# Moving the summing of adaLN modulation rows to VectorE, and into later stages, in a two-layer diffusion trunk

## The chip, the cores and the metric

The kernel runs on 1 core of one Trainium2 chip. The metric is the device time of one execution, in microseconds (us). Engines are called TensorE (PE, its weight loads PEld), VectorE (DVE), ScalarE (ACT), GpSimd (POOL) and SyncE (SP, which issues most transfers).

## What is computed

A trunk of two layers over 1024 latent tokens and 256 context tokens with 1024 features. Layer 0 mixes with a gated short convolution and latent attention, layer 1 with banded windowed attention; each layer ends in a mixture of 16 experts. Every sub-layer is shifted, scaled and gated by modulation rows: six rows of 1024 values per layer, for latent tokens (from `c`) and, where they are needed, for context tokens (from `c_ctx`). Cut to this:

```python
mod = jax.nn.silu(c) @ mod_w[layer] + mod_b[layer]            # 1024 -> 6 x 1024
sh1, sc1, g1, sh2, sc2, g2 = jnp.split(mod[:, None, :], N_MOD, axis=-1)
modc = jax.nn.silu(c_ctx) @ mod_w[layer] + mod_b[layer]       # the same for the context
h = modulate(rms_norm(xs, norm1_g[layer]), sh1, sc1)          # rows 0, 1
...                                                           # y: the mixer of h and hc
xs = xs + g1 * y                                              # row 2
h2 = modulate(rms_norm(xs, norm2_g[layer]), sh2, sc2)         # rows 3, 4
xs = xs + g2 * ec_moe(h2, ...)                                # row 5
```

`mod_w` is 2 x 1024 x 6144 in float32, 50 MB: each row of a layer is a product of one vector with a 4 MB matrix.

## The kernel before

The program runs in stages, one after the other: layer 0's input projection with the convolution (`layer0_conv`), latents, latent attention, output projection with router (`mixer_out`), experts of layer 0 (`moe`), then the same for layer 1.

**Modulation rows.** A row is the sum over 1024 inputs of weight times `silu(c)`. There are two ways to make one. `Part` takes two rows at a time for both kinds of tokens on TensorE: eight pieces of 128 inputs x 2048 features (1 MB each), each used by four products of 32 x 512 (`Part.use`, L299). `Row` takes one row on VectorE: a piece holds 2 x 128 inputs x 1024 features (1 MB); for each 128 inputs and kind of tokens one operation multiplies 128 x 1024 weights by a value per partition and adds them to an accumulator `modacc` (L348; L350 for the first). At its end a few products with ones add over the partitions (`Row.sum`, L356), the bias `modb` is added and GpSimd's queue stores the row in `modr`. The first two rows of layer 0 are a `Part` before everything else. The rest, rows 2 to 5 of layer 0 and 0 and 1 of layer 1 as three `Part`s, and rows 2 to 5 of layer 1 as four `Row`s for latent tokens alone, is a generator (`modulations`), advanced by one piece after nearly every projection of the convolution (`next(rest, None)` in `proj`), with its weights loaded two pieces ahead into the common ring of 1 MB buffers (`raw`).

**Convolution.** Four chunks of 384 columns; per chunk and group of 256 tokens three projections of 24 products each (`pc`), read by ScalarE or VectorE from four PSUM banks. Written order on every queue (`manual_schedule`).

**Output projection.** Tiles of 128 tokens, written order on every queue. In `steps(j)` a tile's 48 products `pw` come in two halves. Beside them run: for the tile before, `xn` of its second half (L1202, L1203), its store to `acc_x`, nine products later its transposes (L1237), then the norm (`nss` to `rr`, eleven short operations), `mul` (L1218), `add` (L1222), store of `h2x`; for the tile itself `xn` of the first half, once the first 24 products are done, and nine products later the first transposes of that. `yl` is the split of the next tile's input. Tile 1 has one more operation, `o.scale(0)`.

**Experts of layer 0.** Per expert twelve weight chunks of 1 MB. Each is loaded into the ring (seven buffers in this stage), cast by ScalarE (`wh`, L1080) and its rest made by VectorE (`wl`, L1081), four buffers deep, and used by three products per block (`pg`, `pu`, `pd`). Context tokens use the raw chunk itself (`pcg`, `pcd`), which frees it. `sil`, `hl`, `xl`, `yo` are VectorE's other operations. In this loop the order on each queue is set by the scheduler, which places instructions by priority in the order of the program and by a model of when their operands are ready. `early()` reads layer 1's rows 0, 1, 3, 4 back at expert 1.

Of the kernel before, what the change touches and what calls it, by code (L numbers as in the profile page):

```python
# [21 lines left out]
D = 1024  # L22
# [17 lines left out]
# one step of the software pipeline of an attention: (operation, how many steps late)  # L40
# [55 lines left out]
def hybrid_block_kernel(ctx, tc, A, out, dbg=None, upto=99):  # L96
# [13 lines left out]
    def psum(name, **tags):  # L110
        """PSUM of a phase: tag -> (buffers, banks each)"""
# [21 lines left out]

    warm = const.tile([128, 1], F32, name="warm")
# [32 lines left out]
    def rstd_steps(pool_, ss, n, dim, tag, out=None):  # L167
        """1/sqrt(ss/dim + eps) for ss [128, n]: the root of dim times 1/sqrt(ss + dim*eps). A generator"""
# [42 lines left out]
    def scale_rows(pool_, l, s, i, g):  # L211
        """norm_g * (1 + sc) on all partitions"""
# [8 lines left out]
    def columns(c, n, scratch, tag):  # L221
        """n rows of D features with the features on partitions: c [128, row, 8]"""
# [4 lines left out]
    class Ring:  # L227
        """buffers for what is read from DRAM, in turn"""
# [4 lines left out]
        def more(self, raws):  # L233
            """further buffers, next in turn"""
# [11 lines left out]
    class Ahead:  # L246
        """the output projection of the first layer in four parts, the first of them split ahead"""
# [29 lines left out]
    class Part:  # L277
        """two of the rows, for latent and context tokens, 512 features at a time, summed by TensorE"""
# [31 lines left out]
        def units(self):  # L310
            def load(k):
                if k == 5:
                    self.load_b()
                self.load(k)

            def use(k):
                self.use(k)
                if k == 7:
                    self.sum()
                    self.store()  # L320

            return [(partial(load, k), partial(use, k)) for k in range(8)]

    class Row:
        """one of the rows, for the kinds of tokens ss, summed by VectorE but over the partitions"""

        def __init__(self, c, l, r, ss, pool_):
            self.c, self.l, self.r, self.ss, self.pool = c, l, r, ss, pool_
            self.w = {}

        def load(self, k):
# [5 lines left out]
            w = self.w[k] = ring.tile([128, 2, D])  # L337
            sp.dma_start(w, A["mod_w"][self.l, k * 128:(k + 2) * 128, self.r * D:(self.r + 1) * D].rearrange("(k p) n -> p k n", p=128))

        def use(self, k):  # L340
# [3 lines left out]
            for i in range(2):  # L344
                for s, a in zip(self.ss, self.acc):
                    cv = self.c[:, 2 * (k + i) + s:2 * (k + i) + s + 1]
# [5 lines left out]
        def sum(self):  # L352
            n = 64 * len(self.ss)
            pm, mb = bank("C", "pm"), self.mb
# [8 lines left out]
        def units(self):  # L363
            return [(partial(self.load, k), partial(self.use, k)) for k in range(0, 8, 2)] + [(None, self.sum)]

    def modulations(parts, rows, ahead):
        """a generator that stops after every piece of the weights, loaded some pieces ahead"""
        a, b = [[u for x in xs for u in x.units()] for xs in (parts, rows)]
        todo = sorted([((i + 0.5) / len(x), i, u) for x in (a, b) for i, u in enumerate(x)], key=lambda t: t[0])
        todo = [u for _, _, u in todo]  # L370
# [15 lines left out]

    def transposes8(src, n=8):
        """eight [128,128] blocks of src (free) into two banks"""
# [8 lines left out]
    # ================= layer 0: projections =================  # L397
    def layer0_conv(hp, wp, cp):
        """first norm, input projection and short convolution"""
        hT = [[hp.tile([128, 8, 256], F32R, name=f"hT{g}_{i}") for i in range(2)] for g in range(5)]  # L400
        csil = hp.tile([128, 16], F32, name="csil")
# [9 lines left out]
        class Group:  # L411
            """256 tokens"""
# [14 lines left out]
            def norm(self):  # L427
                """a generator"""
# [16 lines left out]
            def T(self, b, tag="B"):  # L445
                """two blocks of 128 features of the normalized tokens, features on partitions"""
# [26 lines left out]
        class Chunk:  # L473
            """columns of the input projection, 256 features at a time"""
# [23 lines left out]
        def aside():  # L498
            """the next of the small operations that run between others"""
# [55 lines left out]
        rest = modulations([Part(cs, l, i, cp) for l, i in PARTS], [Row(csil, l, r, ss, cp) for l, r, ss in ROWS], 2)  # L555
# [1874 lines left out]
```

## Time and profile before

| | us |
|---|---|
| median of 3 runs | 2926.6 (2924.9 to 2929.13) |
| span of the profiled execution | 2924.6 |
| TensorE busy | 2732.1 (93%) |
| VectorE busy | 2126.5 (73%) |
| ScalarE busy | 1609.2 (55%) |
| GpSimd busy | 443.8 (15%) |

The profiled execution's own time is its span, 2924.6, and what lies around it, about 2 us by the median. Busy time of TensorE is modelled, so a full TensorE is not TensorE at its peak. The granted clock is a share of 2.4 GHz: 1.00 is that, 0.50 is 1.2 GHz. Start times are from the span's start.

### The profile page before, as it was taken

The page shows a single profiled execution, that of the slowest core. Times are in us where ns is not written, and L with a number is a line of the kernel's source. Part 1 is how long each engine was busy: PE and PEld are TensorE (multiplying, and loading weights), DVE is VectorE, ACT ScalarE, POOL GpSimd, SP SyncE. Part 2 cuts the span into 40 slices and gives each one's busy share as a digit, 9 for nine tenths or more (in the row PEclk, how much of TensorE's full clock was granted, in tenths as well). Part 3 has the DMA queues.
Part 4 walks back from the last instruction along what each step waited for, and adds up shares of the span by engine and source line. Part 5 has one row for each costly group of instructions (what it writes and reads, how often), then busy time and mean ns, then how long its engine had stood idle before and what let it go on. Part 6 is the DMA issues. An engine that isn't in the chain of part 4 may idle for free. (4 is left out here: it accounts for less than half of the span.)

```text
span 2924.6 us, 43411 instructions
## 1 busy us (share of the span) xinstructions
PE 2732.1 (93%) x16999; PEld 2160.2 (74%) x16999; DVE 2126.5 (73%) x3298; ACT 1609.2 (55%) x2390; POOL 443.8 (15%) x293
## 2 busy tenths in 40 slices
PE   6999899999959999999999899899998599999996
PEld 5889899988746666666666678688877488877775
DVE  4653799986666666666666554799976688888887
ACT  4201577773225555555555543588943377776664
POOL 2100100000050111010011210232200622221103
PEclk8999999999979999999999999799999799999998
DMA  7782000016438878788888631310056599999994
GB/s 266 286 317 88 5 8 10 9 60 232 159 111 311 290 275 276 273 290 273 276 270 276 227 126 73 128 37 30 25 192 239 197 377 384 383 382 370 367 354 144
DMA packets 274637, 613.91 MB, mean 210 GB/s; under 512 B 25064, under 2 KB 72928, under 8 KB 270336
## 3 DMA queue, kind: packets, MB, share of 16 engines
q1 hardware_dynamic: 259408, 567.38, 54.2%
q0 software_dynamic: 14880, 43.62, 5.8%
q8 instruction: 134, 2.20, 0.3%
q14 instruction: 71, 0.58, 0.1%
q10 hardware_dynamic: 144, 0.13, 0.0%
HBM read 549.41 MB, written 61.67 MB: 209 GB/s over the span
## 5 line engine op out<-in xcount | busy, mean ns | idle before, releaser
L1081 DVE TENSOR_TENSOR wl<-raw,wh 128x2048 fp32r<-128x2048 f32 (+1 forms) x382 | 861.9, 2283 | 247.7 <-ACT wh L1080 247.6
L1080 ACT CAST wh<-raw 128x2048 fp32r<-128x2048 f32 (+1 forms) x392 | 735.5, 1903 | 260.9 <-PE pg L1723 150.2
L1719 PE MATMUL pg<-wl,xh 128*128 128x512 f32 x512 | 210.0, 410 | 3.6 <-ACT xh L159 2.9
L1721 PE MATMUL pu<-wl,xh 128*128 128x512 f32 x512 | 206.1, 402 | 5.3 <-DVE wl L1081 5.3
L1720 PE MATMUL pg<-wh,xh 128*128 128x512 f32 x512 | 203.2, 397 | 0.0
L1724 PE MATMUL pu<-wh,xl 128*128 128x512 f32 x512 | 202.5, 395 | 0.0
L1723 PE MATMUL pg<-wh,xl 128*128 128x512 f32 x512 | 201.8, 394 | 0.0
L1722 PE MATMUL pu<-wh,xh 128*128 128x512 f32 x512 | 201.6, 394 | 0.0
L1775 PE MATMUL pd<-wl,hh 128*128 128x512 f32 x480 | 197.1, 411 | 1.2
L1776 PE MATMUL pd<-wh,hh 128*128 128x512 f32 x480 | 194.0, 404 | 0.0
L1664 POOL DMA_INDIRECT xg<-h2x,gp x32 | 56.5, 1766 | 721.9 <-PE ptr L393 710.1
L1779 PE MATMUL pd<-wh,hl 128*128 128x512 f32 x480 | 151.2, 395 | 0.0
L1739 ACT ACTIVATE sil<-pg 128x512 f32<-128x512 f32 x64 | 38.3, 598 | 204.3 <-PE pg L1723 204.3
L163 PE MATMUL pc<-hT,wh 128*128 128x256 f32 x480 | 139.8, 291 | 5.5 <-ACT wh L487 3.8
L1789 POOL DMA_INDIRECT acc_x<-yo,gp x30 | 92.9, 3096 | 312.4 <-DVE yo L1788 302.2
L164 PE MATMUL pc<-hT,wh 128*128 128x256 f32 x480 | 135.0, 281 | 0.0
L165 PE MATMUL pc<-hT,wl 128*128 128x256 f32 x480 | 134.9, 281 | 0.0
L1719 PEld LDWEIGHTS pg<-wl,xh 128*128 128x128 f32 x512 | 96.5, 188 | 44.9 <-issue 21.6
L1736 PE MATMUL pcg<-raw,cT 128*32 128x256 f32 x2048 | 125.5, 384 | 0.5 <-DMA raw<-in_exp_w_up_dram 0.5
L1775 PEld LDWEIGHTS pd<-wl,hh 128*128 128x128 f32 x480 | 90.1, 188 | 43.6 <-issue 18.9
L1721 PEld LDWEIGHTS pu<-wl,xh 128*128 128x128 f32 x512 | 96.7, 189 | 32.8 <-DVE wl L1081 10.8
L943 ACT CAST pt<-ppt 128x512 fp32r<-128x512 f32 (+1 forms) x192 | 95.1, 516 | 39.0 <-PE ppt L936 36.8
(437 smaller groups left out, 6638.4 us busy)
## 6 DMA issues: line engine op xcount, KB each, us to landing
raw<-in_exp_w_gate_dram SPq DMA_DIRECT2D x128, 1024.0 KB
raw<-in_exp_w_up_dram SPq DMA_DIRECT2D x128, 1024.0 KB
raw<-in_exp_w_down_dram SPq DMA_DIRECT2D x128, 1024.0 KB
raw<-in_mod_w_dram SPq DMA_DIRECT2D x48, 1024.0 KB
yT<-yTd SPq DMA_DIRECT2D x17, 512.0 KB
acc_x<-xn SPq DMA_DIRECT2D x16, 512.0 KB
h2x<-h SPq DMA_DIRECT2D x16, 512.0 KB
raw<-in_w_in_dram SPq DMA_DIRECT2D x8, 768.0 KB
```

The lines of the kernel that those rows point to most:

```text
L163: pe.matmul(o, ah, bl, start=first, stop=False)
L1080: act.copy(wh[:, cs], raw[:, cs])
L1081: (eng or dve).tensor_sub(wl[:, cs], raw[:, cs], wh[:, cs].bitcast(F32))
L1719: pe.matmul(pg, xh[:, k], gl[:, j], start=k == 0, stop=False)
L1720: pe.matmul(pg, xh[:, k], gh[:, j], start=False, stop=False)
L1721: pe.matmul(pu, xh[:, k], ul[:, j], start=k == 0, stop=False)
L1722: pe.matmul(pu, xh[:, k], uh[:, j], start=False, stop=False)
L1723: pe.matmul(pg, xl[:, k], gh[:, j], start=False, stop=k == 7)
L1724: pe.matmul(pu, xl[:, k], uh[:, j], start=False, stop=k == 7)
L1775: pe.matmul(pd[n], hh[k // 4][:, k % 4], w[2][:, k % 2, ns], start=k == 0, stop=False)
L1776: pe.matmul(pd[n], hh[k // 4][:, k % 4], w[1][:, k % 2, ns], start=False, stop=False)
L1779: pe.matmul(pd[n], hl[k // 4][:, k % 4], w[1][:, k % 2, ns], start=False, stop=k == 7)
```

## The change

`Part` stays for the first two rows alone. All others become `Row`s, spread over three stages:

- convolution: rows 3, 4, 2 of layer 0, for both kinds of tokens, 1 MB pieces, two ahead; the generator is advanced by two of seven projections instead of by each;
- output projection: row 5 of layer 0, for both kinds, in pieces of 128 inputs (512 KB) through one buffer `modw`, one ahead; advanced twice per tile from tile 1 on;
- experts of layer 0: rows 0, 1 (both kinds) and 3, 4, 2, 5 (latent) of layer 1, pieces of 1 MB from the expert ring, one ahead; advanced three times per expert from expert 1 on. Accumulators and bias lie in tiles that the last expert needs later (`lent`). `early()` moves from expert 1 to expert 13.

```diff
-PARTS = [(0, 1), (0, 2), (1, 0)]
-ROWS = [(1, r, (0,)) for r in (2, 3, 4, 5)]
+ROWS = [(3, (0, 1)), (4, (0, 1)), (2, (0, 1))]
+ROWS_OUT = [(5, (0, 1))]
+ROWS_NEXT = [(0, (0, 1)), (1, (0, 1)), (3, (0,)), (4, (0,)), (2, (0,)), (5, (0,))]
...
-            w = self.w[k] = ring.tile([128, 2, D])
+            w = self.w[k] = self.tile([128, self.n, D])
...
-            for i in range(2):
+            for i in range(self.n):
...
-        rest = modulations([Part(cs, l, i, cp) for l, i in PARTS], [Row(csil, l, r, ss, cp) for l, r, ss in ROWS], 2)
+        rest = modulations([Row(0, r, ss, cp, ring.tile, "C") for r, ss in ROWS], 2)
+        calls = [0]
...
                 if j or g > 1:
-                    next(rest, None)
+                    calls[0] += 1
+                    if calls[0] % 7 in (1, 4):
+                        next(rest, None)
...
+            mods = iter(())
+            if l == 0:
+                def mod_tile(shape):
+                    return wp.tile(shape, F32, tag="modw", bufs=1, name="modw")
+
+                mods = modulations([Row(0, r, ss, wp, mod_tile, "B", 1) for r, ss in ROWS_OUT], 1)
...
+                next(mods, None)
                 for _ in range(9):
                     next(m0)
                     yield
+                next(mods, None)
                 y.T(1)
...
+            mods = modulations([Row(1, r, ss, lent, W.tile, "B") for r, ss in ROWS_NEXT], 1) if l == 0 else iter(())
...
+                        if e and c:
+                            steps(mods, 1)
...
-                if e == 1 and early:
+                if e == 13 and early:
...
+                if e:
+                    steps(mods, 1)
                 wd = [W.get(pool if e == E - 1 and c % 2 else None) for c in range(4)]
```

Three places show what moves. First TensorE in the convolution, at the end of a projection and the start of the next; `pm` is a piece of a `Part`, `pc` the projection. Before:

```order
L163 MATMUL pc<-hT_1_109,wh 128x256
L164 MATMUL pc<-hT_0_108,wh 128x256
L165 MATMUL pc<-hT_0_108,wl 128x256
L299 MATMUL pm<-raw,cs 32x512 x4
L163 MATMUL pc<-hT_1_111,wh 128x256
L164 MATMUL pc<-hT_0_110,wh 128x256
L165 MATMUL pc<-hT_0_110,wl 128x256
```

Now no such piece stands between projections; only the end of a row still does, here the first of three:

```order
L166 MATMUL pc<-hT_1_116,wh 128x256
L167 MATMUL pc<-hT_0_115,wh 128x256
L168 MATMUL pc<-hT_0_115,wl 128x256
L346 MATMUL pm<-modacc,ones 32x512 x4
L166 MATMUL pc<-hT_1_118,wh 128x256
L167 MATMUL pc<-hT_0_117,wh 128x256
L168 MATMUL pc<-hT_0_117,wl 128x256
```

24 groups of four products left this queue.

Second the output projection, tile 2, on VectorE: `xn` of the second half of tile 1 and the start of its norm; its `mul` and `xn` of tile 2's first half come behind. Before:

```order
L1202 TENSOR_TENSOR xn<-pw,g_7592 128x512
L1203 TENSOR_TENSOR xn<-xn,xt 128x512
L1213 TENSOR_TENSOR nss<-ss 128x1
L172 TENSOR_SCALAR v<-nss 128x1
L174 TENSOR_SCALAR y<-v 128x1
```

Now:

```order
L1194 TENSOR_TENSOR xn<-pw,g_7438 128x512
L1195 TENSOR_TENSOR xn<-xn,xt 128x512
L338 SCALAR_TENSOR_TENSOR modacc<-modw,csil,modacc 128x1024 x4
L1205 TENSOR_TENSOR nss<-ss 128x1
L175 TENSOR_SCALAR v<-nss 128x1
L177 TENSOR_SCALAR y<-v 128x1
```

SP's queue in the same tile, before:

```order
L1206 DMA acc_x<-xn 128x1024
L1176 DMA xt<-in_xin_dram 128x1024
L1232 DMA h2x<-h_7850 128x1024
L1071 DMA raw<-in_exp_w_up_dram 128x4x512
L1171 DMA yT<-yTd 128x8x128
```

Now:

```order
L1198 DMA acc_x<-xn 128x1024
L1168 DMA xt<-in_xin_dram 128x1024
L328 DMA modw<-in_mod_w_dram 128x1024 x2
L1224 DMA h2x<-h_7712 128x1024
L1063 DMA raw<-in_exp_w_up_dram 128x4x512
L1163 DMA yT<-yTd 128x8x128
```

Two pieces, two operations each, stand in one row on VectorE; `modw` is one buffer, so the first of SP's two loads waits for the first two operations and the last two operations wait for that load.

Third VectorE in the experts of layer 0, from the last chunk of an expert to the `sil` of the next. Before:

```order
L1081 TENSOR_TENSOR wl<-raw,wh 128x2048 x2
L1788 SCALAR_TENSOR_TENSOR yo<-pd,gp,g_8330 128x512 x2
L1687 SCALAR_TENSOR_TENSOR yc<-pcd,cgv,cg_8332 128x256
L1081 TENSOR_TENSOR wl<-raw,wh 128x2048 x3
L1740 TENSOR_TENSOR sil<-sil,pu 128x512
L1081 TENSOR_TENSOR wl<-raw,wh 128x2048
```

Now, from expert 2 to expert 3 (`modacc_10148` and `modacc_10149` are the sums for latent and context tokens):

```order
L1073 TENSOR_TENSOR wl<-raw,wh 128x2048
L340 TENSOR_SCALAR modacc_10148<-raw,csil 128x1024
L340 TENSOR_SCALAR modacc_10149<-raw,csil 128x1024
L338 SCALAR_TENSOR_TENSOR modacc_10148<-raw,csil,modacc_10148 128x1024
L1795 SCALAR_TENSOR_TENSOR yo<-pd,gp,g_8223 128x512 x2
L1689 SCALAR_TENSOR_TENSOR yc<-pcd,cgv,cg_8225 128x256
L338 SCALAR_TENSOR_TENSOR modacc_10149<-raw,csil,modacc_10149 128x1024
L338 SCALAR_TENSOR_TENSOR modacc_10148<-raw,csil,modacc_10148 128x1024
L338 SCALAR_TENSOR_TENSOR modacc_10149<-raw,csil,modacc_10149 128x1024
L338 SCALAR_TENSOR_TENSOR modacc_10148<-raw,csil,modacc_10148 128x1024
L338 SCALAR_TENSOR_TENSOR modacc_10149<-raw,csil,modacc_10149 128x1024
L1073 TENSOR_TENSOR wl<-raw,wh 128x2048 x2
```

Five accumulations stand ahead of the first `wl` of expert 3.

## Rows read from the trace of the kernel before

**Rows 1.** Windows, convolution: length, busy us (instructions) per engine, clock, DMA share, GB/s

```profile
100.00:120.00 20.00, 20.00 (x162) 16.70 (x165) 9.71 (x18) 3.43 (x5) 1.41 (x2) 1.00 1.02 386
140.00:160.00 20.00, 20.00 (x161) 16.12 (x160) 10.42 (x13) 0.37 (x1) 0.53 (x1) 1.00 0.84 321
```

**Rows 2.** Waits of PE, 50 to 240 us: waiter, releaser, us in total, times, longest

```profile
PE pxn L453 <- DVE t L183: 0.6, 1, 0.6
```

**Rows 3.** Timeline of PE in the convolution: start, us, engine, line, instruction

```profile
104.50 0.28 PE L164 MATMUL pc<-hT,wh 128*128 128x256 f32 x1
104.62 0.28 PE L165 MATMUL pc<-hT,wl 128*128 128x256 f32 x1
104.83 1.06 PE L299 MATMUL pm<-raw,cs 128*32 128x512 f32 x8
...
106.05 0.28 PE L164 MATMUL pc<-hT,wh 128*128 128x256 f32 x1
```

**Rows 4.** Tile `modacc`: duration in ns min/median/max, first and last start

```profile
L348 DVE SCALAR_TENSOR_TENSOR modacc<-raw,csil,modacc x28: 1273/1285/1636, 85.0 to 224.2; 128x1024 f32<-128x1024 f32 x28
...
L356 PE MATMUL pm<-modacc,ones x16: 592/604/616, 115.6 to 233.5; 128*32 128x512 f32 x16
```

**Rows 5.** Timeline of DVE, one tile of the output projection

```profile
732.03 0.69 DVE L1202 TENSOR_TENSOR xn<-pw,g 128x512 f32<-128x512 f32 x1 [2.24 <-PE pw L1194]
732.76 0.69 DVE L1203 TENSOR_TENSOR xn<-xn,xt 128x512 f32<-128x512 f32 x1
734.24 0.16 DVE L1213 TENSOR_TENSOR nss<-ss 128x1 f32<-128x1 f32 x1 [0.79 <-ACT pw L1209]
...
736.35 1.29 DVE L1218 SCALAR_TENSOR_TENSOR h<-xn,rr,A 128x1024 f32<-128x1024 f32 x1
...
740.49 0.69 DVE L1203 TENSOR_TENSOR xn<-xn,xt 128x512 f32<-128x512 f32 x1
...
745.69 0.69 DVE L1202 TENSOR_TENSOR xn<-pw,g 128x512 f32<-128x512 f32 x1 [2.24 <-PE pw L1194]
```

**Rows 6.** Timeline of PE in the same tile, its two groups of transposes

```profile
733.88 0.60 PE L1237 MATMUL pxT<-ident,xn 128*128 128x128 f32 x4
...
741.61 0.60 PE L1237 MATMUL pxT<-ident,xn 128*128 128x128 f32 x4
```

**Rows 7.** Timeline of SP in the same tile

```profile
733.48 0.32 SPq L1206 DMA_DIRECT2D acc_x<-xn  x1
733.85 0.42 SPq L1176 DMA_DIRECT2D xt<-in_xin_dram  x1
```

**Rows 8.** Windows, one slice of the same tile

```profile
737.00:738.00 1.00, 1.00 (x7) 0.86 (x8) 0.64 (x1) 0.00 (x0) 0.00 (x0) 1.00 0.26 94
```

**Rows 9.** DMA issues, 880 to 1950 us: count, KB each, median us to landing

```profile
xt<-acc_x POOLq DMA_DIRECT2D x6, 512.0 KB, 4.0
```

**Rows 10.** Timeline of PE at the router, idle time before it in brackets

```profile
795.42 0.87 PE L1237 MATMUL pxT<-ident,xn 128*128 128x128 f32 x3 [4.01 <-DVE xn L1203]
```

**Rows 11.** Windows around that idle time

```profile
790.00:796.00 6.00, 1.99 (x10) 1.44 (x9) 5.83 (x31) 0.70 (x2) 0.00 (x0) 0.88 0.90 242
796.00:802.00 6.00, 6.00 (x25) 5.52 (x24) 5.62 (x33) 0.92 (x3) 0.00 (x0) 0.50 0.57 207
```

**Rows 12.** Line 1788, layer 0: ns min/median/max, first and last start

```profile
L1788 DVE SCALAR_TENSOR_TENSOR yo<-pd,gp,g x30: 740/744/753, 906.6 to 1610.5; 128x512 f32<-128x512 f32 x30
```

**Rows 13.** Windows: an expert's period in layer 0, and 40 us of layer 1's experts

```profile
1000.00:1050.30 50.30, 50.22 (x366) 33.89 (x355) 33.24 (x23) 27.91 (x25) 4.66 (x3) 1.00 0.83 279
2400.00:2440.00 40.00, 40.00 (x185) 32.20 (x184) 35.20 (x24) 28.00 (x21) 8.23 (x2) 1.00 1.04 383
```

**Rows 14.** Waits of DVE in the experts of layer 0, 880 to 1650 us

```profile
DVE wl L1081 <- ACT wh L1080: 195.3, 91, 4.2
DVE sil L1740 <- ACT sil L1739: 55.9, 30, 4.0
```

**Rows 15.** Waits of PE in the experts of layer 1, 2320 to 2860 us

```profile
PE pu L1721 <- DVE wl L1081: 4.7, 7, 0.7
```

More of the change, by code (lines that the diff above doesn't have):

```diff
@@ L132, in hybrid_block_kernel @@
     act.copy(identb, ident)
+    csil = const.tile([128, 16], F32, name="csil")
     warm = const.tile([128, 1], F32, name="warm")
@@ L308, in store, with __init__ @@
                                self.mb[16 * s::32, :])
[L310 to L322, printed above, removed]
     class Row:
-        def __init__(self, c, l, r, ss, pool_):
-            self.c, self.l, self.r, self.ss, self.pool = c, l, r, ss, pool_
+        def __init__(self, l, r, ss, pool_, tile, tag, n=2):
+            self.n = n
+            self.l, self.r, self.ss, self.pool, self.tile, self.tag = l, r, ss, pool_, tile, tag
             self.w = {}
@@ L343, in use @@
             w = self.w.pop(k)
[L344 removed]
+            for i in range(self.n):
                 for s, a in zip(self.ss, self.acc):
[L346 removed]
+                    cv = csil[:, 2 * (k + i) + s:2 * (k + i) + s + 1]
                     if k + i:
@@ L353, in sum @@
             n = 64 * len(self.ss)
-            pm, mb = bank("C", "pm"), self.mb
+            pm, mb = bank(self.tag, "pm"), self.mb
             for j in range(2 * len(self.ss)):
@@ L363, in units, with modulations @@
         def units(self):
[L364 to L370, printed above, removed]
+            return [(partial(self.load, k), partial(self.use, k)) for k in range(0, 8, self.n)] + [(None, self.sum)]
+    def modulations(rows, ahead):
+        todo = [u for x in rows for u in x.units()]
         loads = [load for load, _ in todo if load]
@@ L385, in steps @@
             next(gen, None)
+    steps_of = steps
     def transposes8(src, n=8):
@@ L400, in layer0_conv @@
         hT = [[hp.tile([128, 8, 256], F32R, name=f"hT{g}_{i}") for i in range(2)] for g in range(5)]
-        csil = hp.tile([128, 16], F32, name="csil")
         sp.dma_start(csil, A["cvec"])
@@ L1391, in more @@
                         W.load(1)
+            steps_of(mods, 9)
             fill = more()
@@ L1650, in spread, with moe @@
             return p
-    def moe(l, h2x_, acc_x_, routed, W, gates2, extra, last, early=None, then=None, finish=None):
+    def moe(l, h2x_, acc_x_, routed, W, gates2, extra, last, early=None, then=None, finish=None, lent=None):
         gi, gv, xgs = {}, {}, {}
@@ L2227, in hybrid_block_kernel, with tile, last @@
         lp = st1.enter_context(sbuf("last0"))
-        last = Last(lp.tile([128, 1], F32, name="idf"), lp.tile([128, NX], F32R, name="pick"),
-                    [lp.tile([128, D], F32R, name=n) for n in ("lyh", "lyl")])
+        class Lent:
+            def tile(self, shape, dtype, tag, **_):
+                return lp.tile(shape, dtype, tag={"modacc0": "lyh", "modacc1": "lyl", "modbr": "pick"}[tag], bufs=1, name=tag)
+        lasts = []
+        def last():
+            lasts.append(Last(lp.tile([128, 1], F32, name="idf"), lp.tile([128, NX], F32R, tag="pick", bufs=1, name="pick"),
+                              [lp.tile([128, D], F32R, tag=n, bufs=1, name=n) for n in ("lyh", "lyl")]))
+            return lasts[0]
         w_qkv = []
@@ L2255, in ahead @@
                 load_qkv()
-        moe(0, h2x, acc_x, routed, W, gates2, EX[0], lambda: last, early, ahead)
+        moe(0, h2x, acc_x, routed, W, gates2, EX[0], last, early, ahead, lent=Lent())
     if upto < 5.5:
         return
-    pre = layer1_mixer(st1, last, load_qkv, w_qkv, cols, x_first)
+    pre = layer1_mixer(st1, lasts[0], load_qkv, w_qkv, cols, x_first)
     if upto < 7:
```

2 lines of the change are left out of this document (1 added, 1 removed).

## The prediction

> **What bounds the kernel now.** I read three stretches, since the change touches only these: first busy time by windows, then who waited for whom, then the timelines. In the convolution TensorE is busy 20.00 us of every 20 at full clock while VectorE works about half the time [rows 1], and between 50 and 240 us TensorE waits only once, 0.6 us [rows 2]. The pieces of the modulation summed by TensorE stand in that full stream, so they cost TensorE's time and nothing else. In the output projection a tile is a fixed dance of TensorE and VectorE in hand-written order [rows 5 to 7]. In the experts of layer 0 TensorE is busy 50.22 us of 50.3, VectorE 33.24 [rows 13]; an expert takes (1610.5 - 906.6) / 14 = 50.3 us by the first and last of its output rows [rows 12].
>
> **Convolution: what goes.** A piece is four products, eight records. The last product of the projection before one starts at 104.62, the second one after it at 106.05, where two steps of 0.12 would do: 1.43 - 0.24 = 1.19 us [rows 3]. All 24 pieces after the first part lie in this stretch: 24 x 1.19 = 28.6 us go. Of the summing products at a row's end there were four groups and are three; its records last 604 ns each [rows 4], so I price a group like a piece, and another 1.2 go: -29.8.
>
> **Convolution: what comes.** VectorE multiplies for two kinds of tokens: 3 rows x 8 x 2 = 48 operations instead of 32, at 1.285 us [rows 4], 16 x 1.285 = 20.6 us more, in blocks of four (5.1 us) where blocks of two (2.6) stood. With half of VectorE free [rows 1] and four banks ahead of it most of this is covered; if the cover were gone all 20.6 would show. A block can delay the split of the next columns just before TensorE wants them, at three places; I take 1.7 in all. Transfers fall from 40 pieces of 1 MB to 12, which TensorE did not wait for. Net -28.1, ends -29.8 and -9.
>
> **Output projection: what comes.** Row 5 of layer 0 now needs 16 operations on VectorE, fed through one buffer of 512 KB. The order shows all four operations of a tile side by side, between the second `xn` and `nss`, and the reload between them on SP. I lay that on the tile that starts at 732.03 [rows 5]. The first two operations run from 733.45 to 736.0 (2 x 1.285). Only then is the buffer free and the next piece issued, behind `acc_x` and `xt`, issued at 733.48 and 733.85 [rows 7], whose packets end near 737.3 (share 0.26 in the slice from 737 to 738 [rows 8]). 512 KB at the 386 GB/s of [rows 1] are 1.4 us, so it lands near 738.7; by the nearest row with a landing, 4.0 us after issue [rows 9], at 740.0. VectorE waits for it in order. Then: two operations 2.57, `nss` to `mul` 2.11 (734.24 to 736.35), `mul` 1.29, the two `xn` 1.41: these end at 746.1 to 747.4. The transposes of `xn`, at 741.61 before [rows 6], wait for them: 4.5 to 5.8 us of TensorE; I take 5.0, nearer to the rate. Were the piece there at once, 733.45 + 5.14 + 4.81 = 743.4 leaves 1.8. That is tiles 2 to 4.
>
> Tile 1 has one piece only, but issues its load late, after `xt`, and has one more operation of 1.29: 738.7 + 1.5 + 6.1 = 746.3, stall 4.7 (0 if the piece were there, 5.8 by the slower landing). In tile 5 TensorE reaches the sum after nine products, where 733.88 stands now [rows 6], and the last piece is summed at 736.0: 2.1 us and 1.2 for the products themselves, 3.3. Together 4.7 + 15.0 + 3.3 = 23.0 (8.7 to 26.5). Queued behind VectorE's wait: the norm, `mul`, `xn`, the split `yl` of the next tile; behind SP's: the store of `h2x`, one weight chunk, the next `yT`, all of them early by several us.
>
> A stall of this size also touches TensorE's clock. After the 4.01 us of idle that end at 795.42 the granted clock is 0.88 and then 0.50, the lower of its two levels, for the next 6 us [rows 10, 11]: 3 us lost. Four stalls at that price are 12; whether every such stall lowers the clock this one case can't tell, so I take half, 6 (0 to 12).
>
> The Trainium skill ("TensorE: Matmul & The Clock Gate", section "HAM oscillation — how this bites in real kernels") says that a loop which waits for a transfer in every pass can pay for the lowered clock in every pass. By that rule the clock's term would be 12, not 6; the trace agrees as far as the one idle stretch of [rows 10, 11] can. The Trainium skill ("Trainium Kernel Development and Optimization", section "Best Practices") asks for double buffers, to overlap transfers with work. By that rule, with a second buffer for the pieces, the three tiles would cost 5.4 and not 15; no row here shows this loop with two.
>
> **Experts of layer 0: what comes.** Six rows of layer 1, in 24 pieces of 1 MB: 2 rows x 16 operations for both kinds of tokens, then 4 x 8. TensorE gets six sums, 6 x 1.19 = 7.1 us, in a stretch where it has no idle time: all of it shows. VectorE gets 64 x 1.285 = 82 us. The first two rows fall into experts 1 to 3, about 13.7 each: 33.24 + 13.7 = 46.9 of 50.3; the others spread over some eight experts, 33.2 + 5.1. What VectorE waits for now is the cast by ScalarE (195.3 us) and `sil` (55.9) [rows 14], 16.7 per expert; the second, 3.7 per expert, is a chain that a full queue can't use well, and 46.9 + 3.7 is just over the period. So I charge 1 us in each of these three experts. For the rest the nearest row is layer 1's experts: VectorE 35.20 of 40, 383 GB/s, TensorE 40.00 [rows 13], with 4.7 us of waits for the split in 540 us [rows 15]. Here 279 GB/s plus 3 MB per 50 us is about 340, below that. I charge 6 for these. Each piece also takes one of seven weight buffers until VectorE has used it; that is in the 6. Total 7.1 + 9 = 16.1; ends 7.1, and 48 if all 41 us of the first two rows show because the queue has nothing left to give.
>
> **Sum.** -28.1 + 23.0 + 6 + 16.1 = +17.0. The profiled execution spans 2924.6 and the median of the runs is 2926.6, 2 us around it: 2924.6 + 17.0 + 2 = 2943.6, I say 2943.
>
> **Rivals.**
> *The reload is hidden.* If the piece lands before VectorE asks (a shorter landing than any row has, SP free), the output projection costs 8.7 and no idle long enough for the clock: -28.1 + 8.7 + 7.1 + 5 = -7, 2919. It ends on the other side, and decides once projection and experts together cost under 22. For it: SP and DMA are nearly idle late in a tile. Against: the buffer itself is freed only at 736.0, 5.6 us before the transposes. 0.13.
> *The experts hide everything, and the clock holds.* -28.1 + 23.0 + 7.1 = +2, 2929. Layer 1's rows speak for it; the blocks of five operations ahead of a split, in the order, speak against. 0.13.
> *VectorE becomes the bound of experts 1 to 3.* -28.1 + 23.0 + 6 + 48 = +49, 2976. For: 46.9 of 50.3; against: those casts wait for buffers, not for work. 0.14.
> *The clock stays low through tiles 1 to 4,* since each has an idle stretch like that of [rows 10]. A tile of 13.66 us (732.03 to 745.69) at half clock takes 27.3, 8.6 over the 18.7 already counted; 4 x 8.6 = 34 in place of 6: 2971. For: the four stalls are as long as that one; against: between them TensorE works for some 13 us. 0.08. [...]
> *The convolution doesn't get shorter by what TensorE sheds,* since the blocks of four bind VectorE: -9 in place of -28.1, 2962. [Rows 1] speak against. 0.04.
> *Forecast* (2932 to 2958): 0.48.
>
> **How the numbers follow.** A measurement of this kernel can tell about 0.2%, 5.9 us. Faster than 2920.7: the first rival, 0.13. Within: the second, and the near edge of the forecast, 0.15. Slower: 0.72. The range reaches from just below the hidden reload to the experts' bound: 2918 to 2976 leaves out half of the first rival, a part of the third and little else.
>
> **What would show it.** Convolution: no four-product pieces, TensorE still at 20 of 20, its end some 28 us earlier. Output projection: an idle stretch of 4 to 6 us before the transposes in tiles 1 to 4, ended by `xn`, and VectorE waiting for the `modw` transfer; clock below 1 there. Experts: a period of 50.3 that grows by 2 to 4 us in experts 1 to 3 and by about 1 afterwards, TensorE waiting for splits. I am wrong if tiles 2 to 4 keep 13.7 us, or if an expert grows by more than 8 us.

## The result, and the profile after

The changed kernel takes 2962.8 us (median of 4 runs, 2960.0 to 2967.3), the kernel before 2926.4 beside it: ratio 1.0127, 95% interval 1.0113 to 1.0141. It is slower, as forecast and inside the range, but by 36 us and not by 17. The profiled execution spans 2958.2 us (mean granted clock 0.96) against 2924.6. Its stages, each from the first instruction of its first product to that of the next stage:

| stage (first product) | before, us | after, us | change | forecast |
|---|---|---|---|---|
| up to the convolution (`pc`) | 36.7 | 35.3 | -1.4 | - |
| convolution (`pc` to `pl`) | 226.6 | 202.7 | -24.0 | -28.1 |
| latents (`pl` to `po`) | 107.5 | 109.5 | +2.0 | 0 |
| attention (`po` to `pw`) | 292.0 | 291.0 | -0.9 | 0 |
| output projection (`pw` to `pg`) | 178.8 | 219.2 | +40.4 | +29 with the clock |
| experts of layer 0 (`pg` to `pqkv`) | 827.8 | 845.7 | +17.9 | +16.1 |
| layer 1 | 1255.3 | 1254.8 | -0.5 | 0 |
| sum | 2924.6 | 2958.2 | +33.6 | +17.0 |

How far a stage can move by itself is seen in the kernels below that leave it as it is in the changed kernel: output projection 216.2 to 219.2 us, experts 845.7 to 854.1, layer 1 1254.6 to 1261.3.

**Convolution.** Windows of the changed kernel, which answer to [rows 1] (length, busy us and instructions of PE, PEld, DVE, ACT, POOL, clock, DMA share, GB/s):

```profile
100.00:120.00 20.00, 20.00 (x169) 20.00 (x168) 14.52 (x22) 3.80 (x6) 0.79 (x1) 1.00 0.39 126
140.00:160.00 20.00, 20.00 (x169) 20.00 (x168) 17.62 (x27) 2.04 (x4) 0.56 (x1) 1.00 0.83 299
```

TensorE stays full, VectorE goes from 10 to 15 or 18 us of 20, the transfers shrink: all as forecast. The second column, the weight loads, goes from 16 to 20.00 of 20 because no piece stands between the projections any more: the kernel before shows 20.00 there too from 240 to 260 us, where its pieces are done. Yet the convolution got shorter by 4.1 us less than forecast; a section below looks for the reason.

**Output projection.** The second groups of transposes in tiles 1 to 4, from the timeline of PE; in brackets the idle time before them and what ended it ([rows 6] has one at 733.88 without a bracket):

```profile
670.50 1.09 PE L1229 MATMUL pxT<-ident,xn 128*128 128x128 f32 x4 [7.39 <-DVE xn L1195]
...
692.40 1.09 PE L1229 MATMUL pxT<-ident,xn 128*128 128x128 f32 x4 [6.28 <-DVE xn L1195]
...
717.07 1.09 PE L1229 MATMUL pxT<-ident,xn 128*128 128x128 f32 x4 [8.13 <-DVE xn L1195]
...
738.43 1.09 PE L1229 MATMUL pxT<-ident,xn 128*128 128x128 f32 x4 [5.17 <-DVE xn L1195]
```

That is the wait that was forecast, at its place and with its releaser, but 27.0 us in all and not 19.7. Tile 2 in the timeline of VectorE, to lay beside [rows 5]:

```profile
677.62 2.47 DVE L338 SCALAR_TENSOR_TENSOR modacc<-modw,csil,modacc 128x1024 f32<-128x1024 f32 x2
685.15 2.48 DVE L338 SCALAR_TENSOR_TENSOR modacc<-modw,csil,modacc 128x1024 f32<-128x1024 f32 x2 [5.06 <-DMA modw<-in_mod_w_dram]
...
689.65 1.28 DVE L1210 SCALAR_TENSOR_TENSOR h<-xn,rr,A 128x1024 f32<-128x1024 f32 x1
690.85 0.68 DVE L1194 TENSOR_TENSOR xn<-pw,g 128x512 f32<-128x512 f32 x1
691.57 0.69 DVE L1195 TENSOR_TENSOR xn<-xn,xt 128x512 f32<-128x512 f32 x1
```

and in that of SP's queue, as in [rows 7]:

```profile
677.73 0.34 SPq L1198 DMA_DIRECT2D acc_x<-xn  x1
678.12 0.42 SPq L1168 DMA_DIRECT2D xt<-in_xin_dram  x1
680.12 7.87 SPq L328 DMA_DIRECT2D modw<-in_mod_w_dram  x2
```

The buffer comes free at 680.1, the piece is issued at 680.12 and is there at 685.15: 5.03 us. In tiles 1, 3 and 4 it is 8.1 (655.09 to 663.16), 5.8 (704.07 to 709.82) and 3.9 us (727.24 to 731.17). It comes so late because more stands ahead of it than `acc_x` and `xt`. SP has issued the store of `h2x`, a 1 MB weight chunk and `yT` from 672.65 on, and from 673 to 683 the transfer engines are full (share 0.99, 338 GB/s); then the bytes end:

```profile
683.00:684.00 1.00, 1.00 (x6) 0.82 (x5) 0.00 (x0) 0.00 (x0) 0.00 (x0) 1.00 0.67 270
684.00:685.00 1.00, 1.00 (x6) 0.82 (x5) 0.00 (x0) 0.00 (x0) 0.00 (x0) 1.00 0.05 20
```

VectorE goes on 1.4 us after that; in tiles 1, 3 and 4 it is 1.5, 1.4 and 0.9. In tile 1 the stage's first loads stand ahead of the piece, in tile 3 four loads of the bias as well. Windows around the wait in tile 2, as in [rows 11]:

```profile
686.00:692.00 6.00, 0.12 (x1) 0.00 (x0) 5.62 (x15) 0.00 (x0) 0.00 (x0) 0.92 0.27 87
692.00:698.00 6.00, 5.60 (x16) 4.59 (x17) 2.53 (x3) 1.31 (x3) 0.00 (x0) 0.51 0.43 130
```

TensorE idles, and when its operand is there the granted clock is at its lower level until 697.9. The records show such a fall in each of tiles 1 to 4, while TensorE waits: from 667.2, 691.1, 711.6 and 735.5 on, for 6.8, 6.8, 10.2 and 6.8 us. By the starts of the second `xn` of neighbouring tiles the periods are 23.8, 22.8, 24.3, 21.0 and 16.8 us where 13.7 stood: +9.3, +9.1, +10.6, +7.3, +3.2 (the first against 14.5).

**Experts of layer 0.** 400 us of it, first in the kernel before and then in the changed one (windows, columns as above):

```profile
900.00:1300.00 400.00, 399.36 (x2847) 271.30 (x2847) 268.87 (x191) 221.66 (x199) 42.97 (x26) 1.00 0.83 280
```

```profile
900.00:1300.00 400.00, 384.64 (x2747) 263.79 (x2738) 319.78 (x235) 213.51 (x188) 48.41 (x32) 1.00 0.92 320
```

TensorE is no longer full; VectorE has a fifth of its time left. What waited there is in the list of waits of the changed kernel, 858 to 1703 us (waiter, releaser, us in total, times, longest):

```profile
ACT wh L1072 <- DMA raw<-in_exp_w_gate_dram: 35.1, 7, 19.6
ACT wh L1072 <- DMA raw<-in_exp_w_up_dram: 32.6, 10, 14.4
ACT wh L1072 <- DMA raw<-in_exp_w_down_dram: 32.0, 11, 6.0
...
PE pcd L1790 <- DMA raw<-in_exp_w_down_dram: 8.1, 3, 3.1
```

ScalarE, which casts the expert weights, waited 99.7 us for weights that were not there; in the kernel before such waits came to 3.4 us. And in the list for SP's queue:

```profile
SPq L1063 <- DVE modacc L338: 40.7, 11, 9.9
```

SP, with a weight chunk to load, stood 40.7 us before a ring buffer that VectorE had still to sum out of. By the first output rows of each expert the added time lies in experts 2, 3 and 4 (+2.4, +3.6, +6.1), 6 (+4.5) and 9 (+5.6), some others get shorter, and from expert 11 on, when the rows are done, the period is within 0.7 us of the old one. The forecast had 2 to 4 us in each of experts 1 to 3 and about 1 afterwards. Its 16.1 us came out nearly right, though its parts, as the experiments show, did not.

### The profile page after: what moved, and what is told of

It reads as the page before. It is cut to its first block, busy times and chain, and to the rows that moved or that the text cites. A ratio compares the mean times of both kernels' runs of the same rounds, so it can differ in the third digit from the quotient of the medians.

```text
span 2958.2 us, 43251 instructions
## 1 busy us (share of the span) xinstructions
PE 2720.8 (92%) x16855; PEld 2171.2 (73%) x16855; DVE 2229.2 (75%) x3397; ACT 1608.3 (54%) x2390; POOL 450.0 (15%) x299
## 5 line engine op out<-in xcount | busy, mean ns | idle before, releaser
L1727 PE MATMUL pu<-wh,xl 128*128 128x512 f32 x512 | 201.4, 393 | 0.0
L1201 ACT ACTIVATE pw<-xn 128x512 f32<-128x512 f32 x36 | 21.7, 602 | 202.3 <-DVE xn L1195 202.1
L1722 PEld LDWEIGHTS pg<-wl,xh 128*128 128x128 f32 x512 | 96.5, 188 | 44.4 <-issue 16.1
L1724 PEld LDWEIGHTS pu<-wl,xh 128*128 128x128 f32 x512 | 96.6, 189 | 36.4 <-DVE wl L1073 13.8
L338 DVE SCALAR_TENSOR_TENSOR modacc<-raw,csil,modacc 128x1024 f32<-128x1024 f32 x98 | 121.4, 1278 | 1.4 <-DMA raw<-in_mod_w_dram 1.1
```

Of the source, the lines that this page charges most:

```text
L1722: pe.matmul(pg, xh[:, k], gl[:, j], start=k == 0, stop=False)
L1724: pe.matmul(pu, xh[:, k], ul[:, j], start=k == 0, stop=False)
L1727: pe.matmul(pu, xl[:, k], uh[:, j], start=False, stop=k == 7)
```

## Experiments

The time of each, and its stages in the profiled execution. A ratio is to runs of the kernel before on the same chip.

| kernel | median, us | ratio, 95% interval | convolution | output projection | experts 0 |
|---|---|---|---|---|---|
| changed | 2962.8 | 1.0113 to 1.0141 | 202.7 | 219.2 | 845.7 |
| two_buffers | 2944.1 | 1.0038 to 1.0077 | 203.5 | 195.5 | 846.2 |
| early_two | 2940.9 | 1.0040 to 1.0071 | 202.6 | 190.1 | 852.9 |
| row5_conv | 2934.2 | 1.0011 to 1.0039 | 210.0 | 180.8 | 849.8 |
| no_next | 2940.8 | 1.0029 to 1.0062 | 203.0 | 216.6 | 824.7 |
| sums_only | 2946.9 | 1.0060 to 1.0091 | 203.0 | 216.3 | 832.8 |
| own | 2954.6 | 1.0096 to 1.0127 | 203.6 | 216.2 | 837.1 |
| pad64 | 2970.6 | 1.0135 to 1.0163 | 203.4 | 216.9 | 854.1 |
| before_pad | 2926.1 | 0.9998 to 1.0016 | 226.8 | 179.3 | 824.8 |
| half_own | 2917.5 | 0.9963 to 0.9985 | 205.1 | 179.1 | 839.9 |
| half_own_part | 2924.9 | 0.9983 to 1.0001 | 216.6 | 179.9 | 837.1 |
| apart64 | 2914.6 | 0.9956 to 0.9978 | 201.4 | 176.1 | 835.8 |
| apart32 | 2916.2 | 0.9955 to 0.9980 | 201.6 | 179.3 | 838.8 |

### Output projection: reload or sums?

**two_buffers**

```diff
-                    return wp.tile(shape, F32, tag="modw", bufs=1, name="modw")
+                    turns[0] += 1
+                    if turns[0] % 2:
+                        return wp.tile(shape, F32, tag="modw", bufs=1, name="modw")
+                    return w_out.pool.tile(shape, F32, tag="yT0", bufs=1, name="modw")
...
-                mods = modulations([Row(0, r, ss, wp, mod_tile, "B", 1) for r, ss in ROWS_OUT], 1)
+                mods = modulations([Row(0, r, ss, wp, mod_tile, "B", 1) for r, ss in ROWS_OUT], 2)
```

> Output projection with two buffers for the pieces of row 5 (the second is the place of the first tile's input, which is free by then), loaded two pieces ahead; same sums at the same places. Theory (what costs there is the reload of the one buffer, 5.0 to 6.9 us behind queued transfers, and the clock that falls while TensorE waits for it): tiles 1 to 4 take at most 16 us instead of 21.0 to 24.3, the clock does not fall in them, the stage falls from 219 to about 190 us, about 2933 us in all. Rival (VectorE's two blocks of sums in a tile, 2.6 us each, make the wait by themselves and the clock falls anyway): tiles 1 to 4 keep 19 us or more, the stage 205 or more, 2949 or more.

(Code cut: the tile `yT0` gets a tag, so that its place can be used again.) Tiles 2 to 4 fall to 15.1, 15.2 and 15.2 us, and the clock holds in them. The wait for `xn` from 676 to 760 us, and the window of tile 2:

```profile
PE pxT L1229 <- DVE xn L1195: 3.4, 3, 1.1
```

```profile
676.00:692.00 16.00, 14.87 (x77) 12.22 (x76) 12.68 (x21) 3.57 (x7) 0.00 (x0) 1.00 0.80 260
```

The same sums stand at the same places, so the reload was the cost and VectorE's sums were not: with it 9.1, 10.6 and 7.3 us a tile, without it 1.5. Tile 1 stays at 23.8 with a fall of the clock at 669.0, which the expectation had missed: VectorE waits 9.3 us there for the first load, since the generator issues its first loads only when tile 1 first steps it. So the stage comes to 195.5 us and not to 190.

**early_two** adds one line behind that generator, `next(mods)`, ahead of the tiles.

> The kernel with two buffers, and its first two loads started ahead of the tiles instead of in tile 1. Theory (tile 1 of two_buffers took 23.8 us because its load was issued only in that tile, VectorE waiting 9.3 us for it): tile 1 falls to 15 to 16 us like tiles 2 to 4, its fall of the clock at 669 goes, the output projection takes 195.5 - 9 = 186 to 187 us, 2944 - 9 = 2935 us. Rival (the first pieces of this stage land late whenever they are issued, since the stage's own weights and tokens are on the way): tile 1 stays over 20 us.

Tile 1 takes 19.1 us, VectorE's wait is 2.1 us, the stage falls by 5.4 to 190.1, a little over half of the way hoped for; the rival holds in part: a first load issued at 644.0 is there late as well, and tile 1 now has four operations and not two, while the clock falls once (666.8 to 670.2). Of the 11.3 us that remain over the kernel before, 4.6 are in tile 1 and 1.4 to 1.5 in each of tiles 2 to 5.

**row5_conv**

```diff
-ROWS = [(3, (0, 1)), (4, (0, 1)), (2, (0, 1))]
-ROWS_OUT = [(5, (0, 1))]
+ROWS = [(3, (0, 1)), (4, (0, 1)), (2, (0, 1)), (5, (0, 1))]
+ROWS_OUT = []
...
-                    if calls[0] % 7 in (1, 4):
+                    if calls[0] % 5 in (1, 3):
```

> Row 5 is summed beside the convolution too (20 pieces and sums at 22 of its 54 products, instead of 15 at 16), nothing beside the output projection. Theory (VectorE has room in the convolution, 14 of 20 us busy there): the convolution stays at 202.7 us from its first product, or grows by at most 2; the output projection returns to 179 us with no fall of the clock; 2963 - 40 = 2923, up to 2926. Rival (20 us more on VectorE make the products wait for split weights and tokens): the convolution grows by 8 to 15 us, 2931 to 2938. The experts' stage stays as in the changed kernel, 846 us, in both.

The output projection returns to 180.8, but the convolution grows by 7.4 us, near the rival's lower end. Its waits of TensorE, 40 to 250 us, and one window:

```profile
PE pc L168 <- DVE wl L477: 3.0, 2, 2.4
```

```profile
140.00:160.00 20.00, 17.57 (x137) 17.37 (x136) 16.65 (x22) 1.95 (x3) 0.56 (x1) 0.93 0.09 35
```

One 2.4 us wait, ended at 156.74, is for a split that stood behind a block of four sums, in VectorE's timeline:

```profile
150.56 4.86 DVE L338 SCALAR_TENSOR_TENSOR modacc<-raw,csil,modacc 128x1024 f32<-128x1024 f32 x4
155.35 0.47 DVE L577 SCALAR_TENSOR_TENSOR y<-y,cw,pc 128x256 f32<-128x256 f32 x1
155.74 1.82 DVE L477 TENSOR_TENSOR wl<-raw,wh 128x768 fp32r<-128x768 f32 x2
```

The granted clock falls behind it, from 157.3 to 160.7 (0.93 in the window). The other parts of the 7.4 us are a fourth row end (1.2, as in [rows 3]), waits for `hT` that come to 1.0 more, and 1.4 more of a wait at the stage's start (5.1 for 3.7), which varies from kernel to kernel (4.5 in early_two, 5.0 in apart64 below) and has nothing to do with the sums. VectorE has room in the convolution, but not for blocks of 5.1 us wherever they fall.

### Experts: sums, bytes or buffers?

**no_next**: the generator of layer 1's rows is empty, and the rows read are layer 0's (`mod_row` is changed for that; cut here, as in sums_only).

```diff
-            mods = modulations([Row(1, r, ss, lent, W.tile, "B") for r, ss in ROWS_NEXT], 1) if l == 0 else iter(())
+            mods = iter(())
```

> Layer 1's rows are not computed; layer 1 reads rows of layer 0 in their place, so what it computes is not the reference's. All else as in the changed kernel. Theory (the sums beside the experts and their loads cost what the two traces differ by there): the experts of layer 0 fall from 845.7 back to about 828 us, 2963 - 18 = 2945. Rival (the experts pay nothing for the sums, their longer time is carried over from the output projection or from where tiles lie): they stay at 842 or more, 2959 or more.

824.7 us (827.8 in the kernel before, 824.8 in before_pad below): all of the added time is in these rows, 21 us by the stage and 22.0 by the medians.

**sums_only**: the same sums, from a tile that lies there already (cut here: the rows' loads beside the experts are left out).

```diff
+            class Same:
+                def __getitem__(self, i):
+                    return g2
+
-            mods = modulations([Row(1, r, ss, lent, W.tile, "B") for r, ss in ROWS_NEXT], 1) if l == 0 else iter(())
+            mods = modulations([Row(1, r, ss, lent, lambda shape: Same(), "B") for r, ss in ROWS_NEXT], 1) if l == 0 else iter(())
```

> As the changed kernel, but the rows beside the experts are summed from a tile that is there already: none of their weights are loaded, no buffer of the experts' ring is taken, and layer 1 reads rows of layer 0 in their place. Theory (the experts pay for the loads: their ring buffers are held until VectorE has summed them, so expert weights are loaded late): the experts' stage falls from 845.7 to 828 to 832 us, about 2963 - 16 = 2947. Rival (the sums in VectorE's order delay the split of the weights): the stage stays above 840 us, 2957 or more.

832.8 us: the sums cost 8.1 of the 21 (6.1 by the medians), the rival falls.

**own**: the same bytes through one buffer outside the ring, in pieces of half the size, one more step in an expert.

```diff
+            def mod_tile(shape):
+                return mp.tile(shape, F32, tag="modw", bufs=1, name="modw")
+
-            mods = modulations([Row(1, r, ss, lent, W.tile, "B") for r, ss in ROWS_NEXT], 1) if l == 0 else iter(())
+            mods = modulations([Row(1, r, ss, lent, mod_tile, "B", 1) for r, ss in ROWS_NEXT], 1) if l == 0 else iter(())
...
+                if e:
+                    steps(mods, 1)
                 if e + 1 < E:
                     xT = prep(e + 1)
```

(`yc` and `cuc` share a place, to make room.)

> As the changed kernel, but the weights of layer 1's rows go through one buffer of their own, 128 of the contraction at a time, one piece at four places in an expert, and never through the experts' ring; the same sums and bytes. Theory (holding a ring buffer is what costs, not the bytes and not the sums): the experts' stage falls from 845.7 to 828 to 833 us, about 2963 - 15 = 2948. Rival (the bytes beside the expert weights, 300 GB/s and more, delay these wherever they land): the stage stays above 840 us, 2957 or more.

837.1 us, between the two: 8.6 of the 21 (8.2 by the medians) went with the turn in the ring, and 4.3 over sums_only (7.7 by the medians) are left for the bytes, the smaller pieces and the shared place together. The window of before, in own:

```profile
900.00:1300.00 400.00, 397.73 (x2850) 270.51 (x2849) 314.15 (x228) 222.78 (x197) 47.59 (x31) 1.00 0.92 320
```

The same 320 GB/s and the same share of the DMA engines as in the changed kernel, and TensorE is full again (397.73 for 384.64). ScalarE's waits for expert weights from 856 to 1693 us are down to

```profile
ACT wh L1072 <- DMA raw<-in_exp_w_down_dram: 7.8, 3, 5.1
...
ACT wh L1072 <- DMA raw<-in_exp_w_gate_dram: 2.2, 1, 2.2
ACT wh L1072 <- DMA raw<-in_exp_w_up_dram: 1.9, 2, 1.2
```

Each figure of this split is from one execution, and the stage moves by 8.4 us in kernels that leave it as it is, so its parts are rough. What stands clear of that are two groups. The five kernels whose rows take turns in the ring show 845.7 to 854.1 us, TensorE busy 385 to 387 us of the 400 and ScalarE waiting 100 to 111 us for expert weights; the four with a buffer of their own, own and three below, show 835.8 to 839.9 us, 398 to 399 and 6 to 13. Own also sums in portions half as long; what share these have was not tried.

### Convolution: why only 24 us?

Start to start, the projections' products take 0.1167 us in the kernel before and 0.1200 in the changed one (means of over 1100 steps from 40 to 240 us), from the first projection on, whether VectorE sums, does something else or idles. Some 1430 such steps x 0.0033 = 4.7 us: without them the convolution had got shorter by 28.7. In the timeline of PE of the kernel before, six steps in 0.70 us:

```profile
140.02 0.28 PE L163 MATMUL pc<-hT,wh 128*128 128x256 f32 x1
...
140.72 0.28 PE L163 MATMUL pc<-hT,wh 128*128 128x256 f32 x1
```

and in that of the changed kernel, in 0.72:

```profile
140.03 0.28 PE L167 MATMUL pc<-hT,wh 128*128 128x256 f32 x1
...
140.75 0.28 PE L167 MATMUL pc<-hT,wh 128*128 128x256 f32 x1
```

The instructions there are the same. What the change moved is the condition vector `csil` (64 bytes), from behind the tokens `hT` to ahead of them.

**pad64**, in the changed kernel, and **before_pad**, in the kernel before, both add a line behind `warm`:

```diff
     warm = const.tile([128, 1], F32, name="warm")
+    const.tile([128, 16], F32, name="room")
```

> Only an unused tile of 64 bytes is added ahead of the convolution's tokens, which puts them at the distance from a multiple of 128 bytes that they had in the kernel before (96 instead of 32). Theory (the place of the tokens in SBUF sets the pace of the convolution's products): start to start they fall from 0.1200 back to 0.1167 us, the convolution gets 1428 x 0.0033 = 4.7 us shorter, about 2958 us. Rival (the modulation's products that stood between them gave the weight loads room): the pace stays 0.1200 and the time 2963. If other stages are sensitive to where their tiles lie, they move too, either way.

> The kernel before with only an unused tile of 64 bytes ahead of the convolution's tokens, which then lie exactly where the changed kernel has them. Theory (the place sets the pace of the convolution's products): start to start they go from 0.1167 to 0.1200 us, the convolution gets 4.7 us longer, about 2931 us. Rival (something else that the change brings sets the pace, since 64 bytes more in the changed kernel did not bring the old pace back): the pace stays 0.1167 and the time 2926. What other stages gain or lose shows how far 64 bytes reach beyond the convolution.

Neither changes the pace (0.1200 in pad64, 0.1167 in before_pad): where the tokens lie does not set it. pad64 is 8 us slower than the changed kernel, in the experts and layer 1; these moved nearly as far in early_two (852.9) and two_buffers (1260.7), whose code there is the changed kernel's, and the cause stays open.

**half_own** joins row5_conv and own, and sums a piece of the convolution in two steps.

```diff
-            for i in range(self.n):
+            for i in range(self.n) if half is None else [half]:
...
+            if self.tag == "C":
+                return [x for k in range(0, 8, 2) for x in ((None, partial(self.use, k, 0)), (partial(self.load, k), partial(self.use, k, 1)))] + [(None, self.sum)]
...
-                    if calls[0] % 5 in (1, 3):
+                    if calls[0] % 10 not in (3, 6, 9):
```

> All rows of layer 0 beside the convolution (as row5_conv), but summed in halves of a piece, 36 steps of 2.6 us of VectorE instead of 16 of 5.1 us and 4 sums; layer 1's rows beside the experts through one buffer of their own (as own). Theory (in row5_conv the products waited because a whole piece stood ahead of VectorE's splits; in the experts the held ring buffer was half of the cost): convolution 204 to 207 us instead of 210.0, experts 835 to 839, output projection 181; 2934 - 9 - 4 = 2921 us, faster than the kernel before by 0.2%. Rival (VectorE's total work in the convolution binds, in whatever portions): convolution 209 or more, 2926 us, the same as the kernel before.

2917.5 us, faster than both kernels, than the kernel before by 0.26%: the convolution's waits for the split are gone, and it takes 4.9 us less than in row5_conv with the same sums in blocks half as long, 1.4 of them at its start (a wait of 3.7 us again). The output projection is back at 179.1 us, the experts at 839.9.

**half_own_part** sums rows 0 and 1 of layer 1 by TensorE again (cut here: the eight pieces are spread among the rows' steps, and the generator is advanced more often).

```diff
-        rest = modulations([Row(0, r, ss, cp, ring.tile, "C") for r, ss in ROWS], 2)
+        rest = modulations([Row(0, r, ss, cp, ring.tile, "C") for r, ss in ROWS], 2, [Part(cs, 1, 0, wp)])
...
-ROWS_NEXT = [(0, (0, 1)), (1, (0, 1)), (3, (0,)), (4, (0,)), (2, (0,)), (5, (0,))]
+ROWS_NEXT = [(3, (0,)), (4, (0,)), (2, (0,)), (5, (0,))]
```

> As half_own, but rows 0 and 1 of layer 1 are summed by TensorE in the convolution again (8 pieces, 9.5 us), so that only four single rows stay beside the experts. Theory A on the pace of the convolution's products (pieces of the modulation between them keep it at 0.1167 us, without them it is 0.1200): the pace falls back to 0.1167, the convolution is 9.5 - 4.7 = 5 us longer than in half_own. Theory B (something fixed in the program sets it, or something else that the change took away): the pace stays 0.1200 and the convolution is 9 to 10 us longer. Experts in both: two double sums (2.4 us) and 32 of 64 additions fewer, 6 us less than in half_own. So A gives 2920, B 2925 us.

The pace is 0.1200 with the pieces back in the stream, the convolution 11.5 us longer: theory A falls. The eight pieces cost 9.5 and 1.7 us of waits for splits; the experts give back only 2.8, less than these kernels differ by there (835.8 to 839.9). Summing these two rows on VectorE beside the experts is worth 7 us by the medians.

**apart64** and **apart32** put room between the tokens and the split weights.

```diff
+        hp.tile([128, 16], F32, name="room")
         cs = hp.tile([128, 8, 2, 16], F32, name="cs")
```

(8 in place of 16 for apart32.)

> half_own with an unused tile of 64 bytes between the convolution's tokens and its split weights (where the kernel before had the condition vector that the change moved ahead of both). Theory (the distance from the tokens to the weights, both of which TensorE reads, sets the pace of the products: it was 85216 bytes in the kernel before and in before_pad with 0.1167 us, and 85152 in the five changed ones with 0.1200): the pace returns to 0.1167 us, the convolution falls from 205.1 by 4.7 to 200.4 us, 2917.5 - 4.7 = 2913 us. Rival (something else that the change brought, such as the order of instructions): pace 0.1200, 2917 us.

> As apart64 with 32 bytes between them instead of 64, a distance that no kernel had so far. Theory (the distance sets the pace): it is neither tied to 0.1167 nor to 0.1200, and may be either or a third value between 0.107 and 0.125 us; 2903 to 2924 us. Rival (something else sets it): 0.1200 as in half_own, 2917 us.

In apart64 the pace is 0.1170 on average, six steps in 0.70 us:

```profile
139.97 0.28 PE L166 MATMUL pc<-hT,wh 128*128 128x256 f32 x1
...
140.67 0.28 PE L166 MATMUL pc<-hT,wh 128*128 128x256 f32 x1
```

In apart32 it is 0.1176, a third value. The convolution is 3.8 us shorter than in half_own in apart64, though its first products wait 5.0 us there and not 3.7, and 3.6 us shorter in apart32. By the sizes of the tiles the weights lie at the same place in the kernel before and in the changed one, and the tokens in before_pad and in the changed one; so neither place alone sets the pace, and the distance from the tokens to the weights does, as far as these four layouts and apart32 show. In the total the three kernels can't be told apart (intervals above); apart64 is the fastest found, 0.33% below the kernel before, on the same chip 2914.6 for 2923.2.

## Why the prediction was off

By span the change cost 33.6 us for a forecast of 17.0. Of the 16.6 between them 11.4 lie in the output projection, 4.1 in the convolution, 1.8 in the experts and 2.0 in the latents; the other stages give 2.8 back.

**Output projection, +29.0 with the clock against +40.4: the step that failed is the landing of the reload.** Mechanism, place and releaser were right, the size was not. I let the piece land 2.7 us after its issue by the rate and 4.0 by the nearest landing, and chose near the rate; it took 5.0, 5.8 and 3.9 us in tiles 2 to 4 and 8.1 in tile 1, and the waits of TensorE became 27.0 us and not 19.7. The reason is the tile that I laid it on. The one from 732.03 is tile 5, and SP issues no weight chunk ahead of it, so that its queue is empty at 737.3. Tiles 2 to 4 do have a chunk there. Tile 4 of the kernel before, in SP's timeline and in the window in which its bytes end:

```profile
716.53 0.43 SPq L1071 DMA_DIRECT2D raw<-in_exp_w_gate_dram  x1
...
720.20 0.42 SPq L1176 DMA_DIRECT2D xt<-in_xin_dram  x1
```

```profile
726.00:727.00 1.00, 1.00 (x6) 0.84 (x5) 0.86 (x2) 0.00 (x0) 0.00 (x0) 1.00 0.29 115
```

That is 6.1 us after `xt` was issued, where tile 5 has 3.4. The same sum on this tile gives an estimate of 5.3 us (a buffer free at 722.4, the queue's end at 726.3 and 1.4 for the piece), in the middle of what tiles 2 to 4 measured. Tile 1 stands apart: the stage's first loads fill its queue, which the prediction left out.

- **Tile 5** came out at 3.2 for 3.3, by luck: TensorE waited 0.7 us for the sum and not 2.1, and the products took 2.2 and not 1.2. A tile without the reload was priced nearly right (1.5 for 1.8, in two_buffers).
- **The clock, 6 taken, 12 by the upper end.** It fell in all four tiles, not in half, and stayed at the lower level for 6.8 to 10.2 us, not 6. Of the 36.4 us of tiles 1 to 4, 27.0 are waits; the other 9.4 is left for products that ran at the lower clock. The rule of the Trainium skill ("TensorE: Matmul & The Clock Gate", section "HAM oscillation — how this bites in real kernels") that such a loop pays in every pass was the better guide than the half I took. The fourth rival, a clock that stays low throughout, did not come: between the falls the records show full clock.
- **Convolution, -28.1 against -24.0.** The removal of the pieces was priced right (-28.7 without the slower pace), and the cover by VectorE held (TensorE waited 0.6 us for a split). Missing was a term for the pace: 64 bytes that moved from one side of the tokens to the other, 4.7 us. No row of before could price it; the diff did show that a tile changed its pool.
- **Experts, +16.1 against +17.9: near by luck, for partly wrong reasons.** The sums cost 6 to 8 us, near the 7.1 priced for their products. But I put 9 us on VectorE, with the ring buffers "in the 6", and the held buffers alone are about 8, with 4 to 8 more for the rest of the loads. TensorE waited 4.4 us in all for splits, which the forecast made the sign of this cost, and ScalarE 99.7 for weights. VectorE as the bound, the third rival, was 48 and did not come.
- **Rivals.** The hidden reload failed by the reload. The experts that hide everything failed by it too, and by the experts, 17.9 for 7.1. The fifth rival gave 2962 us, which is the time measured, but not by its mechanism: the convolution did get 24.0 us shorter. That the time lies in the range is owed to the room kept for the other rivals.
- **Latents, +2.0, not priced.** The changed kernel shows the lower clock from 291.7 to 298.5, which the kernel before does not. Kernels with the same code up to there, such as no_next and own, show it for 3.4 to 6.8 us and 108.1 to 109.8 us of latents, half_own not at all and 107.1. What brings it there was not tried.

## What to carry to other kernels

A single buffer that is freed, reloaded and waited for within one step of a loop costs the whole landing behind whatever is queued, and then the clock: give it a second place, even one borrowed from a tile that is done. To price such a landing, read the queue in the very pass that it will stand in: one 1 MB chunk ahead of it was worth 2.7 us here. Work that is put "beside" a full engine should bring its own buffers; a turn in somebody else's ring is paid by the loads that the ring was for. And work that moves to a less busy engine goes in portions shorter than the slack of what is queued behind it: row 5's sums made the convolution 7.4 us longer with blocks of 5.1 us (1.4 of it at the start, not by the sums) and 2.5 with blocks of 2.6.

## What the runs showed of the hardware

- The pace of 256-column products with separate weight loads depends on the distance in SBUF from what TensorE streams (`hT`) to what it loads as weights (`wh`, `wl`): 85216 bytes 0.1167 to 0.1170 us (three kernels), 85184 0.1176 (one), 85152 0.1200 (the ten that keep the changed layout). Moving both together by 64 bytes changes nothing. Why, the runs don't say.
- A transfer of 512 KB landed 3.9 to 8.1 us after its issue in one and the same loop, each time 0.9 to 1.5 us after the bytes of everything queued had passed.
- In each of the four tiles in which TensorE waited 5.2 to 8.1 us the granted clock fell to its lower level, for 6.8 to 10.2 us; in four other kernels with the same stage (no_next, sums_only, own, pad64) it fell in all four tiles too, for 3.4 to 6.8 us. With the waits at 1.1 us or less (two_buffers, tiles 2 to 4) it stayed at 1.00.
